# Row sums of weight tiles crossed over the partitions by a product with ones, in pairs, a pair ahead

## The chip, the cores and the metric

The kernel runs on one core of one Trainium2 chip. The metric is device time in microseconds. Before the change it took 1841.36 us (median of 3 runs, 1831.86 to 1842.78).

## The reference, cut to what matters

One layer of a streaming encoder on 1024 prompt frames and 32 running frames, 1024 channels. A normalised input is projected by a wide matrix, attention with per-head forget gates and a causal depthwise convolution of width 31 run beside each other, and both are gated, projected and added to the input.

```python
h = rmsnorm(x, norm_g)
q, k, v, f, ga, ua, ub, gb, ma, mb = split(h @ w_in)      # 1024 columns each, f: 16
u = ua * sigmoid(ub)
o = fox_attend(rmsnorm(q) / 8, rmsnorm(k), v, cumsum(log_sigmoid(f + b_f)))
conv = causal_dwconv(u, w_dw, b_dw)                        # 31 taps per channel
ya = (o * silu(ga)) @ w_pa
yb = (silu(layernorm(conv)) * silu(gb)) @ w_pb
y = x + (sigmoid(ma) * ya + sigmoid(mb) * yb) @ w_out
```

## The kernel before

Each of the groups ua, ub, ga, ma, k, q, gb, mb has eight weight tiles of 1024x128, held as 128 partitions x 1024 elements. One projection is one such tile times all 1056 frames: three chunks c of 352 frames, eight steps kt in each, and in each step three matmuls (L168), since inputs and weights are both split into a high and a low float16 part: wh·xh, wl·xh, wh·xl. One step of three matmuls is a beat; `beat()` counts ticks, runs what `later` has put off to a tick, and hands out the taps of the convolution to VectorE (L355) at a set rate per beat. A projection has 24 beats, so two have 48.

For the split to float16 each weight tile is scaled by a power of two. Four steps make it:

- `stage`: loads the tile (`raw<-wf`, L213, three buffers), and `squares` runs one pass of ScalarE over it that leaves each partition's sum of squares in `tops` (L105).
- The 128 sums lie in 128 partitions. `squares` writes them to DRAM (`s_st<-tops`, L107) and reads them back with all 128 in the row of every partition (`all<-s_st`, L110). Both DMAs are issued by SyncE (SP), whose queue issues in order.
- `sized` takes the largest on VectorE (L114); `power` makes the scale of it (L142, L143), and GpSimd its inverse (L120).
- `fetch` makes the parts: `wh` on ScalarE (L123), `wl` in three pieces on VectorE (L126).

`PREP` places `sized` and `fetch` in the first chunk (steps 3 and 5) of the projection ahead of the tile's own, and `stage` in the second chunk (step 4), for the tile after it. So a tile's sums are asked for about 15 beats after they are formed.

In order of time the program has these stages. The input is normalised and split while the first two tiles, ub and ua, are multiplied (`x_split`). Then come u1 and two quarters of v, u2 and two more quarters of v (L722, whose tiles go the same way as two raw pieces), then u3, eight pairs of k and q with u4, u5 and u6 between them, and u7. A u is the pair of projections ub and ua. Each k or q projection adds three small pairs of products with a block matrix for the norms (`pst`, L841 and L842) which wait for ScalarE (`sqh`, L831) and VectorE (`sql`, L834). Then eight projections ga. Up to there the order of TensorE, VectorE and ScalarE is that of the code; DMAs and GpSimd are placed by a scheduler. In the attention stage only TensorE has the order of the code: 16 heads of eight blocks, each with scores (L1057, L1058), maximum (L1062), exponential (L1065), scaling on GpSimd (L1068), transposes (L1082) and values (L1101), and after each block four beats of 22 filler projections (gb, ma and part of mb) whose single PSUM buffer is emptied by L897. Two more projections and the three output products follow; these don't use the scale.

Of the kernel before, what the change touches and what calls it, by code (L numbers as in the profile page):

```python
# [24 lines left out]
KT = 8  # L25
# [24 lines left out]
WSP = ((0, 3), (3, 6), (6, 8))  # L50
PREP = ((0, 3), (0, 5), (1, 4))
XCH = ((0, 256), (256, 384), (640, 416))


def build(tc, xT, xt, wv, wf, ckT, cv, clT, stT, vec, cst, yT, kT, vO, lfO, cpT, csT):
# [4 lines left out]
    def pool(name, bufs=1, stack=es, **kw):  # L60
        return stack.enter_context(tc.tile_pool(name=name, bufs=bufs, reuse_waits="tile", **kw))
# [13 lines left out]
    s_m = dram.tile([128, TT], F32, name="s_m")  # L75
    s_st = dram.tile([96, 128], F32, name="s_st")

# [13 lines left out]

    class Scaled:


        def __init__(self, raws):
            self.raws = raws
            self.sc = wx.tile([128, 4], F32, name="sc", tag="sc", bufs=8)

        def squares(self, n):
            self.n = n  # L100
            tops = wx.tile([128, 2], F32, name="tops", tag="tops", bufs=4)
            for i, raw in enumerate(self.raws):
                k = raw.shape[1] * raw.shape[2]
                junk = wx.tile([128, 4 * VC], BF16, name="junk", tag="junk", bufs=1)
                nc.scalar.activation(junk[:, :k], raw.rearrange("p a b -> p (a b)"), AF.Square,  # L105
                                     accum_out=tops[:, i:i + 1])
                nc.sync.dma_start(s_st[n + i].rearrange("(p o) -> p o", o=1), tops[:, i:i + 1])  # L107
            self.all = wx.tile([128, 256], F32, name="all", tag="all", bufs=2)
            for i in range(len(self.raws)):
                nc.sync.dma_start(self.all[:, 128 * i:128 * i + 128],  # L110
                                  s_st[n + i].rearrange("(o p) -> o p", o=1).broadcast_to([128, 128]))

        def most(self):
            nc.vector.tensor_reduce(self.sc[:, 0:1], self.all[:, :128 * len(self.raws)], axis=AX.X, op=ALU.max)  # L114
            self.power(self.sc[:, 0:1])

        def power(self, top):
            q, self.s, self.inv = [self.sc[:, i:i + 1] for i in (1, 2, 3)]
            power(q, self.s, top, 77)
            nc.gpsimd.tensor_scalar(self.inv, q, back, 1.0, op0=ALU.mult, op1=ALU.mult)  # L120

        def high(self, wh, raw, ks):
            nc.scalar.mul(wh[:, ks, :], raw[:, ks, :], self.s)  # L123

        def low(self, wl, wh, raw, ks):
            nc.vector.scalar_tensor_tensor(wl[:, ks, :], raw[:, ks, :], self.s, wh[:, ks, :],  # L126
                                           op0=ALU.mult, op1=ALU.subtract)

        def split(self):
            with tc.high_priority(offset=2000):  # L130
                raw, = self.raws
                xhome.append(xhome.pop(0))
                home = xhome[-1]
                wh, wl = [home.tile([128, KT, 128], F16, name=a, tag=a, bufs=2 if home is wp else 1) for a in ("wh", "wl")]
                self.high(wh, raw, slice(0, KT))
                for k0, k1 in WSP:
                    self.low(wl, wh, raw, slice(k0, k1))
            return wh, wl, self.inv

# [44 lines left out]
    def beat():  # L184

        pace["tick"] += 1
        while late and late[0][0] <= pace["tick"]:
            late.pop(0)[2]()
        if taps or chores:
            pace["credit"] += pace["rate"]  # L190
        while pace["credit"] >= 0 and (taps or chores):
            if chores:
                cost, fn = chores.pop(0)
                fn()
            else:
                cost = taps.pop(0)() or 1.0
            pace["credit"] -= cost

    plan = []
    staged = []  # L200
    split = {}
    serial = [0]

    def stage():

        if plan:
            key = plan.pop(0)
            with tc.high_priority(offset=2000):
                if key[0] == "v":
                    rec = Scaled(v_raws(key[1]))  # L210
                else:
                    raw = wx.tile([128, KT, 128], F32, name="raw", tag="raw", bufs=3)
                    nc.sync.dma_start(raw, wf[WIDX[key]])  # L213
                    rec = Scaled([raw])
                rec.squares(serial[0])
            serial[0] += len(rec.raws)
            staged.append((key, rec))

    def sized():

        if staged:
            with tc.high_priority(offset=2000):
                staged[0][1].most()

    def fetch():

        if staged:
            key, rec = staged.pop(0)
            split[key] = split_v(key[1], rec) if key[0] == "v" else rec.split()

    def steps(key, rh, rl, pspool, evac):

        ahead = key in split
        w = split.pop(key) if ahead else split_w(load_raw(key))
# [193 lines left out]
    with tc.high_priority(offset=9000):  # L428
# [9 lines left out]
        idle = xip.tile([128, CH], F16, name="idle")  # L438
        nc.vector.memset(idle, 0.0)
        ones_w = xip.tile([128, 128], F32, name="ones_w")  # L440
        nc.gpsimd.memset(ones_w, 1.0)
        tops = xip.tile([128, 4], F32, name="tops")
        gsq = xip.tile([128, KT], F32, name="gsq")
# [5 lines left out]
        G8 = slice(C_NG, C_NG + KT)  # L449
        recs = [Scaled([raw]) for raw in raws]  # L450
        warm = tr.tile([128, 512], F32, name="warm", tag="tr")
# [117 lines left out]
    def high(i, p):  # L569
        recs[i].high(ws0[i][0], raws[i], slice(*WSP[p]))  # L570

    def low(i, p):
        recs[i].low(ws0[i][1], ws0[i][0], raws[i], slice(*WSP[p]))

# [6 lines left out]
    def known(i):  # L581
        recs[i].power(psq[:, i + 1:i + 2])

# [29 lines left out]

    plan.extend([("ub", 1), ("ua", 1), ("v", 0), ("v", 1), ("ub", 2), ("ua", 2), ("v", 2), ("v", 3), ("ub", 3), ("ua", 3)])
    for f in range(8):
        if f in (2, 4, 6):
            plan.extend([("ub", 3 + f // 2), ("ua", 3 + f // 2)])
        plan.extend([("k", f), ("q", f)])
    plan.extend([("ub", 7), ("ua", 7)] + [("ga", f) for f in range(8)])
    fills = [("gb", f) for f in range(8)] + [(g, f) for g in ("ma", "mb") for f in range(8)]  # L620
    plan.extend(fills)
    x_split(0, ws0, u0, {
# [15 lines left out]
        6: [lambda: scale(5, 1), lambda: scale(7, 1)],  # L638
        7: [lambda: scale(8, 1), stage]})
    x_split(2, ws0, u0, {1: [stage], 3: [consts], 4: [sized], 5: [fetch], 7: [sized]})  # L640
    drain((0, 0))
# [16 lines left out]
    def v_raws(c):  # L658
        raws = [vp.tile([128, 4, VC], F32, name="vraw", tag="vraw", bufs=4) for _ in range(2)]
        for hf in range(2):  # L660
            nc.sync.dma_start(raws[hf], wv[c, :, hf * 4:hf * 4 + 4, :])
        return raws

    def split_v(c, rec):
        wh2, wl2, raws2 = [], [], rec.raws
        for raw in raws2:
            with tc.high_priority(offset=1500):
                wh, wl = [vp.tile([128, 4, VC], F16, name=a, tag=a, bufs=4) for a in ("vwh", "vwl")]
                rec.high(wh, raw, slice(0, 4))
                for k in (0, 2):  # L670
                    rec.low(wl, wh, raw, slice(k, k + 2))
            wh2.append(wh)
            wl2.append(wl)
# [25 lines left out]
    for c in range(4):  # L699
# [13 lines left out]
        pace["rate"] = R_V  # L713
        wh2, wl2, inv = split.pop(("v", c))
        for t in range(8):
            ps = pj.tile([128, 512], F32, name="pjv", tag="pj")
            n = 0
            for kt in range(KT):
# [5 lines left out]
                beat()  # L724
            for at, fn in ((1, sized), (2, fetch), (5, stage)):
                if t == at:
                    fn()
            vf = vp.tile([128, 256], F32, name="vf", tag="vf", bufs=6)
# [224 lines left out]
    psS = pool("psS", 2, stack=p2, space=PS)  # L953
    psT = pool("psT", 3, stack=p2, space=PS)
    ap = pool("ap", 2, stack=p2, side="right")

# [634 lines left out]
```

## Time and profile before

| | us |
|---|---|
| median of 3 runs | 1841.36 |
| the profiled execution | 1837.22 |
| its span | 1835.2 |
| TensorE busy | 1451.8 |
| VectorE busy | 999.2 |
| ScalarE busy | 717.7 |
| GpSimd busy | 442.2 |

The mean granted TensorE clock over the span is 0.887 of full speed. A line such as "DVE sc L114 <- DMA all<-s_st: 501.7, 64, 13.6" in the table of waits reads: VectorE's instructions of line 114 that write `sc` had their engine idle ahead of them until a DMA of `all` from `s_st` ended, 501.7 us in total in 64 cases, the longest 13.6 us. PE is TensorE, PEld its weight loads, DVE VectorE, ACT ScalarE, POOL GpSimd, SPq the queue of SyncE. A matmul's recorded duration reaches over the start of the next, so the rate of matmuls is read from their starts.

### The profile page before, as it was taken

The numbers are of one execution on the slowest core, as the hardware profiler recorded it, in microseconds if no ns is written. First come the engines' busy times: TensorE is split into PE (matmuls) and PEld (weight loads), VectorE is DVE, ScalarE is ACT, GpSimd is POOL, SyncE is SP. The second block draws the span as 40 slices with busy tenths as digits, with TensorE's granted clock in tenths as the row PEclk, the third lists the DMA queues.
The fourth block names the chain that finished last, engine by engine and source line by source line (L and its number), as shares of the span: only waits on it lengthen the run. The fifth ranks groups of instructions, "written<-read, shape, count | busy, mean of one in ns | idle before, by whom it ended". The sixth has DMA issues, their size and how long they took to land.

```text
span 1835.2 us, 25063 instructions
## 1 busy us (share of the span) xinstructions
PE 1451.8 (79%) x9344; PEld 1053.5 (57%) x9344; DVE 999.2 (54%) x1702; ACT 717.7 (39%) x1362; POOL 442.2 (24%) x505
## 2 busy tenths in 40 slices
PE   8797967767777777673676678777768699999999
PEld 5485744434444444441454455455546466999999
DVE  6575655545557676553465464544424253865575
ACT  6433335344354542212243333443424344652331
POOL 1000103122233230001222222212112122564563
PEclk8998988987799888985778888898889899999999
DMA  4442444528344336664233433534434423874453
GB/s 173 77 142 47 125 57 98 83 76 172 55 100 95 88 98 84 83 68 54 67 94 105 89 108 85 115 88 111 96 87 115 110 70 131 306 252 133 132 184 95
DMA packets 133657, 199.61 MB, mean 109 GB/s; under 512 B 45280, under 2 KB 100192, under 8 KB 133536
## 3 DMA queue, kind: packets, MB, share of 16 engines
q1 hardware_dynamic: 133392, 197.94, 44.4%
q8 instruction: 74, 1.21, 0.4%
q14 instruction: 47, 0.39, 0.1%
q10 hardware_dynamic: 144, 0.07, 0.0%
HBM read 132.27 MB, written 65.68 MB: 108 GB/s over the span
## 4 chain that ended last, share of the span: by engine, by line
DMA 47%; PE 28%; DVE 12%; ACT 7%; issue 5%; POOL 0%; SPq 0%; ACTq 0%; DVEq 0%; POOLq 0%
DMA s_st<-tops 29%; PE pj L168 16%; DMA all<-s_st 13%; PE pj L1423 4%; DMA raw<-wf 4%; DVE y L355 3%; PE pjv L722 3%; DVE wl L126 2%; ACT junk L105 2%; DVE nm L1062 2%; ACT wh L123 1%; PE ptr L1082 1%; ACT P L1065 1%; PE po L1101 1%; DVE sc L114 1%
## 5 line engine op out<-in xcount | busy, mean ns | idle before, releaser
L168 PE MATMUL pj<-xh,wh 128*128 128x352 f16 (+2 forms) x1536 | 519.9, 339 | 116.6 <-ACT t L897 54.7
L168 PE MATMUL pj<-xh,wl 128*128 128x352 f16 (+2 forms) x1536 | 518.5, 338 | 3.6 <-DVE wl L126 3.6
L168 PE MATMUL pj<-xl,wh 128*128 128x352 f16 (+2 forms) x1536 | 516.4, 336 | 2.7 <-DVE xl L557 2.4
L168 PEld LDWEIGHTS <-wh 128*128 128x128 f16 x3072 | 322.7, 105 | 259.9 <-ACT wh L123 64.3
L355 DVE SCALAR_TENSOR_TENSOR y<-u,vec_t,y 128x1086 f32<-128x1086 f32 x240 | 332.4, 1385 | 3.4 <-ACT y L352 0.4
L114 DVE TENSOR_REDUCE sc<-all 128x1 f32<-128x128 f32 (+1 forms) x67 | 19.7, 293 | 501.7 <-DMA all<-s_st 501.7
L168 PEld LDWEIGHTS <-wl 128*128 128x128 f16 x1536 | 160.9, 105 | 157.4 <-issue 63.2
L120 POOL TENSOR_SCALAR sc<-sc,back 128x1 f32<-128x1 f32 x69 | 44.7, 648 | 717.9 <-DVE sc L142 682.1
L1068 POOL TENSOR_SCALAR P<-P,nm 128x128 f32<-128x128 f32 (+7 forms) x128 | 120.5, 943 | 314.4 <-DVE nm L1067 272.2
L123 ACT ACTIVATE wh<-raw,sc 128x1024 f16<-128x1024 f32 (+1 forms) x68 | 74.4, 1095 | 306.4 <-DVE sc L143 306.4
L1065 ACT ACTIVATE P<-psS,nm 128x128 f32<-128x128 f32 (+7 forms) x128 | 94.8, 741 | 247.9 <-DVE nm L1062 190.8
L1057 PE MATMUL psS<-KB,QB 128*128 128x256 f32 (+2 forms) x192 | 89.7, 468 | 109.5 <-ACT P L1065 97.2
L126 DVE SCALAR_TENSOR_TENSOR wl<-raw,sc,wh 128x384 f16<-128x384 f32 (+1 forms) x192 | 105.5, 602 | 29.3 <-ACT wh L123 27.9
L1057 PEld LDWEIGHTS psS<-KB,QB 128*128 128x128 f32 x192 | 40.7, 212 | 129.5 <-ACT P L1065 104.9
L1082 PE MATMUL ptr<-ident,P 128*128 128x128 f32 x576 | 93.7, 294 | 9.4 <-DVE ot L1106 4.8
L1062 DVE TENSOR_REDUCE nm<-psS 128x1 f32<-128x128 f32 (+7 forms) x128 | 96.4, 754 | 7.3
L1082 PEld LDWEIGHTS ptr<-ident,P 128*128 128x128 f32 x576 | 77.2, 154 | 17.6 <-POOL P L1068 5.4
L1085 ACT COPY pt<-ptr 128x512 f32<-128x512 f32 (+3 forms) x128 | 64.2, 501 | 57.5 <-PE ptr L1082 56.5
L105 ACT ACTIVATE junk<-raw 128x1024 bf16<-128x1024 f32 x62 | 65.2, 1052 | 54.5 <-DMA raw<-wf 31.0
L859 POOL TENSOR_TENSOR ql<-qn,qh 128x352 fp32r<-128x352 f32 (+1 forms) x48 | 59.5, 1240 | 107.6 <-ACT qh L858 74.5
L722 PE MATMUL pjv<-vwh,xh 128*128 128x260 f16 x256 | 72.2, 282 | 14.3 <-ACT vwh L123 12.5
L160 POOL TENSOR_TENSOR wl<-raw,wh 128x384 fp32r<-128x384 f32 (+1 forms) x51 | 63.1, 1265 | 74.6 <-ACT wh L157 58.8
(266 smaller groups left out, 2628.8 us busy)
## 6 DMA issues: line engine op xcount, KB each, us to landing
raw<-wf SPq DMA_DIRECT2D x92, 512.0 KB
QB<-s_q SPq DMA_DIRECT2D x32, 256.0 KB
KB<-s_k SPq DMA_DIRECT2D x32, 256.0 KB
all<-s_st SPq DMA_DIRECT2D x70, 64.0 KB
kT<-qn SPq DMA_DIRECT2D x8, 528.0 KB
s_ga<-t SPq DMA_DIRECT2D x24, 176.0 KB
s_gb<-t SPq DMA_DIRECT2D x24, 176.0 KB
s_ma<-t SPq DMA_DIRECT2D x24, 176.0 KB
```

What stands on the lines that cost most here:

```text
L105: nc.scalar.activation(junk[:, :k], raw.rearrange("p a b -> p (a b)"), AF.Square, accum_out=tops[:, i:i + 1])
L123: nc.scalar.mul(wh[:, ks, :], raw[:, ks, :], self.s)
L126: nc.vector.scalar_tensor_tensor(wl[:, ks, :], raw[:, ks, :], self.s, wh[:, ks, :], op0=ALU.mult, op1=ALU.subtract)
L168: nc.tensor.matmul(ps, a[:, kt, :], b(kt, sl), start=(first and n == 0), stop=(last and n == N - 1))
L355: t = nc.vector.scalar_tensor_tensor(y, u[:, i:i + CW], w, y, op0=ALU.mult, op1=ALU.add)
L722: nc.tensor.matmul(ps[:, :VC], a, b, start=(n == 0), stop=(n == 23))
L1057: nc.tensor.matmul(ps[:, b, :wm], QB[:, qsl], KB[:, ksl], start=True, stop=False)
L1062: nc.vector.tensor_reduce(nm[:, 0:1], ps[:, :nb, :w], axis=AX.XY, op=ALU.max, negate=True)
L1065: nc.scalar.activation(P[:, :nk].rearrange("p (b w) -> p b w", b=nb), ps[:, :nb, :w], AF.Exp, bias=nm[:, 0:1], accum_out=nm[:, 1:2])
L1068: nc.gpsimd.tensor_scalar(P[:, :nk], P[:, :nk], nm[:, 2:3], 1.0, op0=ALU.mult, op1=ALU.mult)
L1082: nc.tensor.transpose(pt[:, 128 * j:128 * j + 128], P[:, 128 * (4 * u + j):128 * (4 * u + j) + 128], ident)
L1423: nc.tensor.matmul(pss[c][:, :HC], a[:, k, :], x, start=(not more and kt == 0 and n == 0), stop=(kt == 3 and n == 2), skip_group_check=more)
```

## The change

The class `Scaled` becomes `Batch`, which stands for two tiles (a quarter of v: one batch of two raw pieces with one common scale). The sums of squares go to `topb` in bfloat16 on GpSimd, and `total` multiplies a matrix of ones with them on TensorE, which leaves in each partition the sum over all 128 partitions. `power` reads that from PSUM for both tiles at once. The scale thus follows from the total and not from the largest partition. `s_st`, `all` and the maximum go. Where the old kernel had three marks in each projection, `begin` at the start of a pair lists the jobs for the next pair with their ticks, and `beat` runs them. There are four raw buffers.

```diff
-            for i, raw in enumerate(self.raws):
...
-                nc.sync.dma_start(s_st[n + i].rearrange("(p o) -> p o", o=1), tops[:, i:i + 1])
-            self.all = wx.tile([128, 256], F32, name="all", tag="all", bufs=2)
-            for i in range(len(self.raws)):
-                nc.sync.dma_start(self.all[:, 128 * i:128 * i + 128],
-                                  s_st[n + i].rearrange("(o p) -> o p", o=1).broadcast_to([128, 128]))
-
-        def most(self):
-            nc.vector.tensor_reduce(self.sc[:, 0:1], self.all[:, :128 * len(self.raws)], axis=AX.X, op=ALU.max)
-            self.power(self.sc[:, 0:1])
+            raw = wx.tile([128, KT, 128], F32, name="raw", tag="raw", bufs=4)
+            nc.sync.dma_start(raw, wf[WIDX[key]])
...
+                    nc.scalar.activation(junk[:, :raw.shape[1] * raw.shape[2]], raw.rearrange("p a b -> p (a b)"),
+                                         AF.Square, accum_out=self.tops[:, i:i + 1])
+                if len(self.raws) == 2:
+                    nc.gpsimd.tensor_copy(self.topb, self.tops)
+
+        def total(self):
+            pool, tag = totals[-1]
+            self.ps = pool.tile([128, 512], F32, name="tot", tag=tag)
+            if self.n == 2:
+                nc.tensor.matmul(self.ps[:, :2], ones_b, self.topb, start=True, stop=True)
+            else:
+                for i in range(2):
+                    nc.tensor.matmul(self.ps[:, 0:1], ones_b, self.topb[:, i:i + 1], start=(i == 0), stop=(i == 1))
+
+        def power(self, ps=None, n=0):
+            ps, n = (self.ps, self.n) if ps is None else (ps, n)
+            with tc.high_priority(offset=2000):
+                q, self.s, self.inv = [self.sc[:, 2 * i:2 * i + n] for i in range(3)]
+                power(q, self.s, ps[:, :n], 77)
+                nc.gpsimd.tensor_scalar(self.inv, q, back, 1.0, op0=ALU.mult, op1=ALU.mult)
...
     def beat():
 
         pace["tick"] += 1
+        while prep and prep[0][0] <= pace["tick"]:
+            prep.pop(0)[1]()
...
+    def begin():
+
+        if not plan:
+            return
+        b = plan.pop(0)()
+        t = pace["tick"]
+        if b.n == 2:
+            jobs = ((3, b.stage), (13, b.stage), (25, b.total), (27, b.power), (29, lambda: b.split(0)),
+                    (40, lambda: b.split(1)))
+        else:
+            jobs = ((3, b.stage), (25, b.total), (27, b.power),
+                    (29, lambda: split.__setitem__(b.keys[0], split_v(b.keys[0][1], b))))
+        prep.extend((t + n, fn) for n, fn in jobs)
...
-                if ahead and (c, kt) in PREP:
-                    (sized, fetch, stage)[PREP.index((c, kt))]()
```

In `x_split` the first pair is loaded and squared at the end of the second chunk and the start of the third, its total follows at step 3 and its splits at steps 5 and 7 of the third chunk. In the attention stage `tot` takes one of the three PSUM buffers of the transposes (`psT`), before that the single buffer `tr`.

VectorE, in the pairs of k and q; before, the maximum of the sums, the scale and three pieces of `wl` of one tile:

```order
L355 SCALAR_TENSOR_TENSOR y<-u,vec_t,y 128x1086
L114 TENSOR_REDUCE sc<-all 128x1
L142 TENSOR_SCALAR sc<-sc 128x1
L143 TENSOR_SCALAR sc<-sc 128x1
L126 SCALAR_TENSOR_TENSOR wl<-raw,sc,wh 128x384 x2
L126 SCALAR_TENSOR_TENSOR wl<-raw,sc,wh 128x256
L848 SCALAR_TENSOR_TENSOR qn<-pj,gi,ri 128x352
```

The same engine after the change, in a later pair of k and q (the lines on `ls`, `csm`, `ch` and `cl` are the small work on the forget gates that falls there):

```order
L158 TENSOR_SCALAR sc<-tot 128x2
L159 TENSOR_SCALAR sc<-sc 128x2
L813 COPY ls<-lfT 16x32
L142 SCALAR_TENSOR_TENSOR wl<-raw,sc,wh 128x384 x2
L142 SCALAR_TENSOR_TENSOR wl<-raw,sc,wh 128x256
L814 SCALAR_TENSOR_TENSOR csm<-on_3443,ls 16x544
L864 SCALAR_TENSOR_TENSOR qn<-pj,gi,ri 128x352
L850 TENSOR_TENSOR sql<-sqf,sqh 128x352
L816 CAST ch<-cc 16x1024
L864 SCALAR_TENSOR_TENSOR qn<-pj,gi,ri 128x352
L817 TENSOR_TENSOR cl<-cc,ch 16x1024
L142 SCALAR_TENSOR_TENSOR wl<-raw,sc,wh 128x384 x2
```

The reduction is gone, the scale comes once for two tiles from `tot` in PSUM, and the two tiles' `wl` stand apart.

SyncE's queue in a pair of k and q, before:

```order
L861 DMA s_k<-ql 128x352
L213 DMA raw<-wf 128x1024
L860 DMA s_k<-qh 128x352
L107 DMA s_st<-tops 128x1
L861 DMA s_k<-ql 128x352
L864 DMA kT<-qn 128x1056
L110 DMA all<-s_st 128x128
L860 DMA s_k<-qh 128x320
L861 DMA s_k<-ql 128x320
```

And after:

```order
L877 DMA s_k<-ql 128x352
L107 DMA raw<-wf 128x1024
L876 DMA s_k<-qh 128x352
L877 DMA s_k<-ql 128x352
L880 DMA kT<-qn 128x1056
L876 DMA s_k<-qh 128x320
L107 DMA raw<-wf 128x1024
L877 DMA s_k<-ql 128x320
```

The write of the sums and their reading back have left the queue, and a second tile is loaded within the same stretch.

TensorE after the change, at the 25th beat of a pair (before, only the rows of L184, then L168, stood there):

```order
L184 MATMUL pj<-xl,wh 128x352
L126 LDWEIGHTS ones_b
L126 MATMUL tot<-topb,ones_b 128x2
L184 LDWEIGHTS wh
L184 MATMUL pj<-xh,wh 128x352
```

One product with its weight load has come into TensorE's own stream; there are 31 such for pairs and two for each of the four quarters of v.

More of the change, by code (lines that the diff above doesn't have):

```diff
@@ L75, in build @@
     s_m = dram.tile([128, TT], F32, name="s_m")
-    s_st = dram.tile([96, 128], F32, name="s_st")
     cp = pool("cp")
@@ L136, in split @@
                 for k0, k1 in WSP:
-                    self.low(wl, wh, raw, slice(k0, k1))
-            return wh, wl, self.inv
+                    self.low(i, wl, wh, raw, slice(k0, k1))
+            split[self.keys[i]] = wh, wl, self.inv[:, i:i + 1]
     def power(q, s, top, e):
@@ L199, in build @@
     plan = []
-    staged = []
     split = {}
[L202 to L229, printed above, removed]
+    prep = []
+    totals = []
+    def begin():
[10 more added lines that the diff above has]
+        prep.extend((t + n, fn) for n, fn in jobs)
     def steps(key, rh, rl, pspool, evac):
-        ahead = key in split
-        w = split.pop(key) if ahead else split_w(load_raw(key))
+        if key in firsts:
+            begin()
+        w = split.pop(key) if key in split else split_w(load_raw(key))
         for c in range(3):
@@ L439, in build @@
         nc.vector.memset(idle, 0.0)
+        ones_b = cp.tile([128, 128], BF16, name="ones_b")
+        nc.vector.memset(ones_b, 1.0)
         ones_w = xip.tile([128, 128], F32, name="ones_w")
         nc.gpsimd.memset(ones_w, 1.0)
-        tops = xip.tile([128, 4], F32, name="tops")
+        tops = xip.tile([128, 4], F32, name="tops0")
         gsq = xip.tile([128, KT], F32, name="gsq")
@@ L449, in build @@
         G8 = slice(C_NG, C_NG + KT)
-        recs = [Scaled([raw]) for raw in raws]
+        recs = [Batch((i,)) for i in range(2)]
         warm = tr.tile([128, 512], F32, name="warm", tag="tr")
@@ L638, in build @@
         6: [lambda: scale(5, 1), lambda: scale(7, 1)],
-        7: [lambda: scale(8, 1), stage]})
-    x_split(2, ws0, u0, {1: [stage], 3: [consts], 4: [sized], 5: [fetch], 7: [sized]})
+        7: [lambda: scale(8, 1), b1.stage]})
+    x_split(2, ws0, u0, {0: [b1.stage], 2: [consts], 3: [b1.total, b1.power], 5: [lambda: b1.split(0)],
+                         7: [lambda: b1.split(1)]})
     drain((0, 0))
@@ L668, in split_v @@
                 wh, wl = [vp.tile([128, 4, VC], F16, name=a, tag=a, bufs=4) for a in ("vwh", "vwl")]
-                rec.high(wh, raw, slice(0, 4))
+                rec.high(0, wh, raw, slice(0, 4))
                 for k in (0, 2):
-                    rec.low(wl, wh, raw, slice(k, k + 2))
+                    rec.low(0, wl, wh, raw, slice(k, k + 2))
             wh2.append(wh)
@@ L714, in build @@
         wh2, wl2, inv = split.pop(("v", c))
+        begin()
         for t in range(8):
@@ L954, in build @@
     psT = pool("psT", 3, stack=p2, space=PS)
+    totals.append((psT, "T"))
     ap = pool("ap", 2, stack=p2, side="right")
```

84 lines of the change are left out of this document (48 added, 36 removed).

## The prediction

> **What bounds the kernel now.** I read the page's chain first, then the table of waits, one round of the timeline, and last the busy times by stage. The page:
>
> ```profile
> span 1835.2 us, 25063 instructions
> DMA 47%; PE 28%; DVE 12%; ACT 7%; issue 5%; POOL 0%; SPq 0%; ACTq 0%; DVEq 0%; POOLq 0%
> DMA s_st<-tops 29%; PE pj L168 16%; DMA all<-s_st 13%; PE pj L1423 4%; DMA raw<-wf 4%; DVE y L355 3%; PE pjv L722 3%; DVE wl L126 2%; ACT junk L105 2%; DVE nm L1062 2%; ACT wh L123 1%; PE ptr L1082 1%; ACT P L1065 1%; PE po L1101 1%; DVE sc L114 1%
> L114 DVE TENSOR_REDUCE sc<-all 128x1 f32<-128x128 f32 (+1 forms) x67 | 19.7, 293 | 501.7 <-DMA all<-s_st 501.7
> L120 POOL TENSOR_SCALAR sc<-sc,back 128x1 f32<-128x1 f32 x69 | 44.7, 648 | 717.9 <-DVE sc L142 682.1
> ```
>
> 42% of the chain that ends last is two tiny DMAs, the write of the row sums and their reading back, and VectorE stands 501.7 us ahead of the 67 maxima. Those waits block a queue in order: every tap, eviction and maximum behind L114 waits too. The table of waits shows who pays, and that SyncE is blocked by the same write:
>
> ```profile
> ACT wh L123 <- DVE sc L143: 306.4, 41, 13.9
> PE psS L1057 <- ACT P L1065: 97.2, 18, 10.2
> PE pst L841 <- ACT sqh L831: 44.7, 14, 7.0
> PE pst L842 <- DVE sql L834: 39.7, 17, 5.7
> SPq L110 <- DMA s_st<-tops: 499.3, 69, 9.6
> ```
>
> One round in order of time (start, duration, engine; in brackets the idle time before):
>
> ```profile
> 461.71 0.32 SPq L107 DMA_DIRECT2D s_st<-tops  x1
> 471.38 0.32 SPq L110 DMA_DIRECT2D all<-s_st  x1
> 471.75 0.31 PE L168 MATMUL pj<-xl,wh 128*128 128x352 f16 x1
> 474.71 0.29 DVE L114 TENSOR_REDUCE sc<-all 128x1 f32<-128x128 f32 x1 [8.20 <-DMA all<-s_st]
> 475.40 1.15 ACT L123 ACTIVATE wh<-raw,sc 128x1024 f16<-128x1024 f32 x1 [5.93 <-DVE sc L143]
> 476.61 0.47 PE L168 MATMUL pj<-xh,wh 128*128 128x352 f16 x1 [4.54 <-ACT wh L123]
> 477.82 0.50 PE L168 MATMUL pj<-xh,wh 128*128 128x352 f16 x1
> 478.11 0.50 PE L168 MATMUL pj<-xh,wl 128*128 128x352 f16 x1
> ```
>
> The write takes 471.38 - 461.71 = 9.67 us, the reading back 474.71 - 471.38 = 3.33, together 13.0. TensorE has used up its tile, waits 4.54 us for the next, and then runs at a start distance of 0.29 us. Busy times by stage (length, then PE, PEld, DVE, ACT, POOL, granted clock, DMA share, GB/s):
>
> ```profile
> 0.00:55.20 55.20, 46.14 (x256) 29.39 (x257) 31.44 (x85) 31.26 (x65) 8.26 (x21) 0.91 0.40 145
> 55.20:133.90 78.70, 69.62 (x562) 53.12 (x560) 49.73 (x66) 30.63 (x66) 6.04 (x7) 0.96 0.46 114
> 133.90:217.30 83.40, 71.57 (x565) 53.92 (x563) 53.37 (x66) 32.04 (x71) 6.35 (x7) 0.94 0.33 95
> 217.30:691.40 474.10, 353.27 (x1979) 213.60 (x1977) 281.10 (x414) 204.16 (x366) 120.15 (x122) 0.86 0.44 93
> 691.40:828.00 136.60, 101.39 (x578) 60.39 (x578) 77.04 (x100) 32.53 (x51) 9.21 (x10) 0.87 0.64 73
> 828.00:1544.00 716.00, 522.62 (x3445) 363.76 (x3445) 329.98 (x747) 275.89 (x597) 144.10 (x218) 0.85 0.38 92
> 1500.00:1544.00 44.00, 43.71 (x360) 30.62 (x360) 20.02 (x46) 20.27 (x44) 7.95 (x13) 1.00 0.15 49
> 1544.00:1565.00 21.00, 21.00 (x143) 13.78 (x142) 9.35 (x16) 11.29 (x14) 5.43 (x6) 1.00 0.87 307
> 1565.00:1835.00 270.00, 266.23 (x1829) 265.48 (x1826) 167.17 (x211) 99.90 (x136) 142.67 (x114) 1.00 0.55 180
> ```
>
> They are x_split; u1 with half of v; u2 with the rest; u3 to u7 with k and q; ga; attention; its last 44 us, where no tile is prepared any more; the last two gates; the output products. Where no sums are fetched TensorE is busy 99 to 100% at clock 1.00. Where they are, it is busy 73 to 75% at 0.85 to 0.87, and no engine is full. So the round trip bounds everything from 55 to some 1465 us.
>
> **The floor.** What would TensorE alone need? 143 matmuls in 21.00 us are 0.147 us each, so a projection of 72 takes 10.6 us. The products of float32 operands at the end run at 270 / 1829 = 0.148; six of them for the norms make a k or q 11.5. For v and the attention:
>
> ```profile
> 107.30 24.95 PE pjv L722 x224
> 1473.75 0.64 PE L1057 MATMUL psS<-KB,QB 128*128 128x256 f32 x1
> 1500.04 0.31 PE L168 MATMUL pj<-xh,wh 128*128 128x352 f16 x1 [0.25 <-ACT t L897]
> 1501.92 1.08 PE L990 MATMUL psS<-kc,qs_t 64*32 64x512 f32 x8
> 1502.80 0.26 PE L991 MATMUL psS<-ks_t,qs_t 64*32 64x32 f32 x8
> 1505.48 0.41 PE L1057 MATMUL psS<-KB,QB 128*128 128x256 f32 x1
> ```
>
> A quarter of v is 192 matmuls at 24.95 / 224 = 0.111, 21.4 us. From the second block of one head to that of the next, after the last wait for sums, go 1505.48 - 1473.75 = 31.7 us, with one of the four groups of running frames in them. So 16 heads take at most 508. Such a group's scores take about 1.1 us (L990 and L991), its transposes and 20 small products some 2 more, an estimate; 12 heads have none, which gives 508 - 36 = 472, and I use 470. Floors by stage: u1 and half of v 21.2 + 42.8 = 64, the same again 64, u3 to u7 with k and q 5 x 21.2 + 16 x 11.5 = 290, ga 85, attention 470.
>
> **The change part by part.**
>
> *The round trip goes.* All 501.7 us of waits on VectorE and 499.3 on SyncE lose their cause, and 67 maxima of 0.293 us go. The Trainium skill's DMA: Bandwidth & Descriptors ("Anatomy of one DMA") gives about 2.0 us of fixed cost to a DMA. Two would be 4.0 us, less than the some 15 beats (15 x 3 x 0.147 = 6.6 us) that the old order leaves them, and the change would gain nothing: 1835. The trace, with 9.67 and 3.33, disagrees, and it decides.
>
> What is late next? In u3 to q7 VectorE: from its 281.10 I take 24 times a maximum and about half the scale work, some 0.4 each, and 270 us are left beside TensorE's 290. An engine in order that is 93% loaded delivers late at times. Of the 84.4 us that L841 and L842 wait now I let half stay, and add 8 for the tiles: 340. ScalarE's 204.16 leave it room. In ga VectorE keeps about 74 of 85: 97.
>
> *Total on TensorE.* 35 batches (31 pairs and four quarters), one or two products each, in TensorE's own queue: behind a waiting total every projection stands. The nearest rows, a product with ones of the first stage, and one load of a tile in the attention with the ScalarE pass that waited for it:
>
> ```profile
> L458 PE MATMUL pj<-tops,ones_w x6: 167/260/353, 5.2 to 12.1; 128*128 128x1 f32 x6
> 865.31 0.33 SPq L213 DMA_DIRECT2D raw<-wf  x1
> 869.91 1.06 ACT L105 ACTIVATE junk<-raw 128x1024 bf16<-128x1024 f32 x1 [0.86 <-DMA raw<-wf]
> ```
>
> Below, 0.26 us a batch, 9 in all; nothing speaks for a gain of its own. Above, the total waits for a load only now issued: 4.60 + 1.06 + 0.65 for the copy on GpSimd (by L120, mean 0.648) + 0.26 = 6.6 us, 230 in all. Between second stage and total lie twelve beats, 5.3 us, and with four buffers the load can start before its stage; SyncE's new order has it there. So I take it nearer to the lower end, some 1.5 us a batch, 35 of them 52 us, which lie within the additions of this sum.
>
> *Pairs.* Both splits stand 19 and 8 beats, 8.4 and 3.5 us, ahead of the pair's end, the second not needed for 24 beats more. In the attention ScalarE makes both `wh` in a row and VectorE six pieces of `wl`, ahead of a block's maximum. For this and the totals I add 45 us there, 3.75 for each of the 12 batches: 515. The first totals add 7 and 5 in the stages of v, where a quarter's load stands behind the stores of u0 in SyncE's queue: 71 and 69. If the cover of twelve beats fails, it is the 230 above. The copy of two numbers on GpSimd and the third and fourth buffer cost nothing that is waited for: GpSimd is busy 120.15 of 474.10 us.
>
> *x_split* has one wait for sums in it and one at its end, which go:
>
> ```profile
> 49.39 0.29 DVE L114 TENSOR_REDUCE sc<-all 128x1 f32<-128x128 f32 x1 [4.11 <-DMA all<-s_st]
> 60.12 0.28 DVE L114 TENSOR_REDUCE sc<-all 128x1 f32<-128x128 f32 x1 [6.19 <-DMA all<-s_st]
> ```
>
> Of their 10.3 us I take 7 off this stage: 48.
>
> Sum: 48 + 71 + 69 + 340 + 97 + 515 + 21 + 270 = 1431 us, against floors of 48 + 64 + 64 + 290 + 85 + 470 + 21 + 270 = 1312. With the 2 us by which the execution (1837.22) exceeds its span: 1433. The median of the runs stands 0.2% above the profiled execution, so 1436; I say 1435.
>
> **The rivals.**
>
> 1. *Nearly the floor.* The pairs hide all; 1312 + 35 = about 1350. For it: 99% busy in 1500 to 1544. Against: no tile is prepared there, and VectorE has 20.02 of 44 to do, not 93%.
>
> 2. *Small waits keep the clock down.* With VectorE and ScalarE closely behind TensorE, a product for the norms, an eviction or a total waits 1 to 2 us a few times in each pair, and the granted clock stays at 0.86 as now. Then 290, 85 and 470 become 845 / 0.86 = 983, 138 more, and with 60 of waits 1312 + 198 = 1510. Against: at 1500.04 a wait of 0.25 left the clock at 1.00. The Trainium skill's TensorE: Matmul & The Clock Gate ("A second HAM failure mode: psum-queue depth-cycling") says that short idle spells between groups of matmuls, as buffers are cycled, let the clock swing. By it the sum would be this rival's 1510; the row of 1500.04 does not bear it out, for waits that short.
>
> 3. *The total is a new wait in full.* 230 us on TensorE, 1312 + 230 + 60 = 1600.
>
> 4. *Slower.* SyncE issues in order. If in the attention a tile's load stands behind a load of V that waits for TensorE's values, while TensorE stands at that tile's total, each batch costs a round of three engines. Slower than now begins where a batch costs (1835 - 1312) / 35 = 15 us, 1850 at 15.4. That is longer than the longest wait of `wh` for its scale, 13.9 us, at every one of 35 batches, and the DMA engines are rid of two transfers a tile.
>
> 5. *The round trip was hidden anyway*, no change: the 4.54 us of TensorE at 476.61, and 306.4 us of `wh`, speak against it.
>
> **How the numbers follow.** Forecast (1375 to 1490) 0.56; near the floor 0.13; small waits 0.17; totals in full 0.08; slower 0.04; no change 0.02. 1345 to 1560 holds the forecast, the second rival, and most of the first: a little over 0.8. Within 1% is about what a measurement here can't tell from no change. Faster by over 1%: 0.56 + 0.13 + 0.17 + 0.08 = 0.94; within 0.02; slower 0.04.
>
> **What would show it.** In the profile of the changed kernel: no `s_st` or `all`; VectorE's idle time ahead of L158 below 60 us in all; TensorE's idle time ahead of the totals (L126, L129) below 60, against some 230 in the third rival; a granted clock of 0.95 or more over the whole span, against 0.86 to 0.90 in the second; u3 to q7 in 310 to 370 us with `pst` as its first waiter; a head of attention in 29 to 34 us. I am wrong if a new wait of TensorE over 100 us appears on one line, or if the stages from 55 us on shrink by less than 300 us together.

## The result and the profile after

The changed kernel took 1402.55 us (median of 4 runs, 1402.31 to 1402.74), beside 1842.07 for the kernel before. The ratio is 0.762 with an interval of 0.760 to 0.765: 24% faster. Of two kernels further down, the unused round trip and the late pairs, only the profiled run is used, since the other run of each was disturbed.

The page of the changed kernel's profiled run (1402.74 us; mean granted clock 0.983):

```profile
span 1401.0 us, 24783 instructions
PE 1331.1 (95%) x9383; PEld 1008.6 (72%) x9383; DVE 983.2 (70%) x1572; ACT 723.8 (52%) x1362; POOL 428.6 (31%) x508
PE 75%; DVE 10%; DMA 6%; ACT 5%; issue 3%; POOL 0%; SPq 0%; ACTq 0%; DVEq 0%; POOLq 0%
```

The chain that ended last was 47% DMA and 28% TensorE; it is now 6% DMA and 75% TensorE. VectorE and ScalarE have nearly the same busy time as before (983.2 and 723.8 us, against 999.2 and 717.7): their work has not become cheaper, they only no longer stand still. The table of waits of the same run, TensorE's, VectorE's on the totals, and those of SyncE's queue:

```profile
PE pst L858 <- DVE sql L850: 24.1, 7, 8.1
PE pj L184 <- ACT t L913: 15.6, 17, 4.7
PE psS L1074 <- ACT P L1082: 10.5, 5, 6.3
DVE sc L158 <- PE tot L126: 18.6, 9, 4.6
DVE sc L158 <- PE tot L129: 2.0, 2, 1.1
SPq L914 <- ACT t L913: 149.2, 40, 9.3
SPq L107 <- DVE wl L142: 138.1, 42, 30.2
```

Where VectorE waited 501.7 us for the sums read back, it waits about 21 for totals. SyncE's longest wait is now for data to be stored (L914, an evicted gate) or for a raw buffer to come free (L107, by the last `wl` that reads it) (the longest of 30.2 us); TensorE's own waits for what lies behind them are the small ones above. Busy times by stage, same columns and stages as in the prediction, without its row for the attention's last 44 us:

```profile
0.00:52.10 52.10, 43.43 (x257) 28.12 (x258) 32.86 (x88) 32.57 (x66) 8.51 (x22) 0.97 0.47 172
52.10:119.30 67.20, 66.56 (x567) 52.15 (x565) 54.13 (x63) 31.63 (x66) 2.05 (x8) 1.00 0.47 150
119.30:186.20 66.90, 66.90 (x570) 52.52 (x569) 48.99 (x57) 33.21 (x71) 4.01 (x9) 1.00 0.30 99
186.20:519.50 333.30, 308.57 (x1993) 200.42 (x1992) 278.28 (x367) 205.77 (x369) 114.56 (x117) 0.96 0.40 124
519.50:606.70 87.20, 86.51 (x583) 56.67 (x581) 75.67 (x83) 37.56 (x57) 6.99 (x16) 1.00 0.36 121
606.70:1109.50 502.80, 471.71 (x3455) 339.26 (x3455) 316.26 (x691) 271.83 (x586) 142.75 (x216) 0.98 0.45 124
1109.50:1130.50 21.00, 21.00 (x143) 13.81 (x142) 9.46 (x16) 11.29 (x14) 5.44 (x6) 1.00 0.86 300
1130.50:1401.00 270.50, 266.44 (x1829) 265.66 (x1826) 167.51 (x211) 99.96 (x136) 144.27 (x114) 1.00 0.56 180
```

| stage | before | predicted | after |
|---|---|---|---|
| x_split | 55.2 | 48 | 52.1 |
| u1, u2 and v | 162.1 | 140 | 134.1 |
| u3 to u7 with k, q | 474.1 | 340 | 333.3 |
| ga | 136.6 | 97 | 87.2 |
| attention | 716.0 | 515 | 502.8 |
| last gates, output products | 291.0 | 291 | 291.5 |
| sum | 1835.0 | 1431 | 1401.0 |

The two stages in which nothing was changed stand still; the gain lies in the others. The clock goes with it: in the stages of v and ga TensorE is now busy 99 to 100% and the granted clock is 1.00, where it was 0.87 to 0.96.

The preparation of one pair of k and q in order of time, picked from the timeline (start, duration, engine):

```profile
377.99 0.33 SPq L107 DMA_DIRECT2D raw<-wf  x1
384.16 0.33 SPq L107 DMA_DIRECT2D raw<-wf  x1
384.65 1.05 ACT L117 ACTIVATE junk<-raw 128x1024 bf16<-128x1024 f32 x1
390.24 1.04 ACT L117 ACTIVATE junk<-raw 128x1024 bf16<-128x1024 f32 x1
393.32 1.28 POOL L120 CAST topb<-tops 128x2 bf16<-128x2 f32 x1
395.52 0.31 PE L184 MATMUL pj<-xl,wh 128*128 128x352 f16 x1
395.67 0.17 PE L126 MATMUL tot<-topb,ones_b 128*128 128x2 bf16 x1
395.70 0.31 PE L184 MATMUL pj<-xh,wh 128*128 128x352 f16 x1
396.97 0.15 DVE L158 TENSOR_SCALAR sc<-tot 128x2 int32<-128x2 int32 x1
397.16 0.17 DVE L159 TENSOR_SCALAR sc<-sc 128x2 int32<-128x2 int32 x1
398.11 1.13 ACT L139 ACTIVATE wh<-raw,sc 128x1024 f16<-128x1024 f32 x1
```

Each load is issued 6 to 7 us ahead of the pass that reads it, and neither pass has to wait. The second row sum was ready at 391.38, when ScalarE's accumulator had been read behind the pass shown, the copy of both at 394.60, and the total goes through TensorE at 395.67 between two matmuls that start 0.18 us apart, against 0.15 elsewhere. From the sums to VectorE's first use of the total the crossing takes 396.97 - 391.38 = 5.6 us, where it took 13.0; some 3 of them are slack ahead of the copy and of the product, TensorE spends 0.17, and in this pair neither TensorE nor VectorE waits for any of it.

### The profile page after: what moved, and what is told of

The parts are those of the page before. It is cut to its first block, busy times and chain, and to the rows that moved or that the text cites. A ratio compares the mean times of both kernels' runs of the same rounds, so it can differ in the third digit from the quotient of the medians.

```text
span 1401.0 us, 24783 instructions
## 1 busy us (share of the span) xinstructions
PE 1331.1 (95%) x9383; PEld 1008.6 (72%) x9383; DVE 983.2 (70%) x1572; ACT 723.8 (52%) x1362; POOL 428.6 (31%) x508
## 4 chain that ended last, share of the span: by engine, by line
PE 75%; DVE 10%; DMA 6%; ACT 5%; issue 3%; POOL 0%; SPq 0%; ACTq 0%; DVEq 0%; POOLq 0%
PE pj L184 50%; PE pjv L741 6%; PE pj L1440 5%; PE po L1118 4%; DMA raw<-wf 4%; DVE y L359 4%; PE ptr L1099 3%; PE psS L1074 2%; DVE nm L1079 2%; PE psS L1075 2%; DVE wl L142 2%; ACT P L1082 1%; ACT wh L139 1%; ACT t L913 1%; PE pst L858 1%
## 5 line engine op out<-in xcount | busy, mean ns | idle before, releaser
L184 PE MATMUL pj<-xh,wh 128*128 128x352 f16 (+2 forms) x1536 | 487.0, 317 | 17.7 <-ACT t L913 15.6
L184 PE MATMUL pj<-xl,wh 128*128 128x352 f16 (+2 forms) x1536 | 485.6, 316 | 1.4 <-DVE xl L563 1.1
L184 PE MATMUL pj<-xh,wl 128*128 128x352 f16 (+2 forms) x1536 | 486.1, 316 | 0.3 <-DVE wl L142 0.3
L184 PEld LDWEIGHTS <-wh 128*128 128x128 f16 x3072 | 304.1, 99 | 164.8 <-issue 4.3
L184 PEld LDWEIGHTS <-wl 128*128 128x128 f16 x1536 | 152.0, 99 | 93.4 <-issue 21.9
L1082 ACT ACTIVATE P<-psS,nm 128x128 f32<-128x128 f32 (+7 forms) x128 | 94.8, 741 | 71.9 <-DVE nm L1079 59.0
L1074 PE MATMUL psS<-KB,QB 128*128 128x256 f32 (+2 forms) x192 | 81.5, 426 | 13.9 <-ACT P L1082 10.5
L120 POOL CAST topb<-tops 128x2 bf16<-128x2 f32 x35 | 15.1, 432 | 233.6 <-ACT junk L117 180.1
L117 ACT ACTIVATE junk<-raw 128x1024 bf16<-128x1024 f32 x62 | 65.2, 1051 | 31.9 <-DMA raw<-wf 31.5
L1084 DVE RECIPROCAL nm<-nm 128x1 f32<-128x1 f32 x128 | 20.5, 160 | 77.8 <-ACT P L1082 76.8
L1118 PE MATMUL po<-pt,V 128*64 128x256 f32 x640 | 72.8, 382 | 0.0
L1077 DVE TENSOR_TENSOR psS<-psS,cmask 128x128 f32<-128x128 f32 x128 | 37.5, 294 | 47.4 <-PE psS L1075 47.0
```

The source lines that it names most:

```text
L184: nc.tensor.matmul(ps, a[:, kt, :], b(kt, sl), start=(first and n == 0), stop=(last and n == N - 1))
L1074: nc.tensor.matmul(ps[:, b, :wm], QB[:, qsl], KB[:, ksl], start=True, stop=False)
L1082: nc.scalar.activation(P[:, :nk].rearrange("p (b w) -> p b w", b=nb), ps[:, :nb, :w], AF.Exp, bias=nm[:, 0:1], accum_out=nm[:, 1:2])
L1118: nc.tensor.matmul(po[rows], V[:, j, :], parts[c][:, j, :], start=(c % 2 == 0 and j < 2), stop=(c % 2 == 1 and j >= 2 * c))
```

## The experiments

Theory A was that the exchange of the crossing carries the whole gain, and that pairs, the pair ahead and the buffers are worth next to nothing by themselves. Against it stood that the larger lead of the pairs hides the round trip, so that it matters little how the sums cross. Within A a second question was open: is it VectorE's waiting for the sums that cost the time, or SyncE's queue, which stands at each store until it has landed (A2)? All kernels compute the whole reference.

### The crossing alone, and the pairs alone

The kernel before, with only the crossing exchanged; single tiles, three buffers and the old marks stay:

```diff
-                nc.sync.dma_start(s_st[n + i].rearrange("(p o) -> p o", o=1), tops[:, i:i + 1])
...
+            nc.gpsimd.tensor_copy(self.topb[:, :m], tops[:, :m])
+
+        def total(self):
...
+            for i in range(m):
+                nc.tensor.matmul(self.ps[:, 0:1], ones_b, self.topb[:, i:i + 1], start=(i == 0), stop=(i == m - 1))
...
-            nc.vector.tensor_reduce(self.sc[:, 0:1], self.all[:, :128 * len(self.raws)], axis=AX.X, op=ALU.max)
-            self.power(self.sc[:, 0:1])
+            self.power(self.ps[:, 0:1])
```

> The kernel before with only the crossing exchanged: product with ones in place of the two DMAs and the maximum; single tiles, three raw buffers and the old marks stay (sums asked for 15 beats after they are formed). Theory A, the round trip itself is what cost: Square 1.05, copy 0.2 to 1.3 and product 0.2 us fit into 15 beats (6.6 us), so nearly the whole gain is here: 1400 to 1440 us. Theory B, the pairs and their place a pair ahead are what hides it: a good part of the gain is missing, 1500 us or more.

It took 1399.26 us (1398.39 to 1402.06), ratio 0.767 (0.765 to 0.769). The changed kernel, run again on another chip beside the kernel before, took 1402.68, ratio 0.769 (0.766 to 0.772).

> The changed kernel unaltered, for comparison on this chip: 1395 to 1410 us.

The crossing alone gives the whole gain, just below the range that theory A gave. The view of its line of totals:

```profile
L116 PE MATMUL tot<-topb,ones_b x71: 163/167/178, 43.5 to 1106.8; 128*128 128x1 bf16 x71
  DVE xl L565: 1.2, 2
  POOL topb L109: 0.5, 1
```

71 totals instead of 39, and TensorE stood ahead of them 1.7 us in all. Its old marks leave some 15 beats between sums and total, and that suffices too. By stage the two kernels are not alike: u3 to u7 take 325.1 us with single tiles and 333.3 with pairs, the attention 507.7 and 502.8, so the pairs lose 8 us in the one stage and gain 5 in the other.

The other half: the changed kernel with the two DMAs and the maximum put back, in pairs, a pair ahead, four buffers:

```diff
+                    nc.sync.dma_start(s_st[serial[0]].rearrange("(p o) -> p o", o=1), self.tops[:, i:i + 1])
+                    nc.sync.dma_start(self.all[:, i, :],
+                                      s_st[serial[0]].rearrange("(o p) -> o p", o=1).broadcast_to([128, 128]))
...
-                nc.tensor.matmul(self.ps[:, :2], ones_b, self.topb, start=True, stop=True)
...
+                        nc.vector.tensor_reduce(ps, self.all, axis=AX.X, op=ALU.max)
```

> The changed kernel with the two DMAs and the maximum put back in place of the product; pairs, their ticks and four raw buffers stay. Theory A: the second tile's sums are asked for 14 beats (6.2 us) after they are formed and need some 13 us, so VectorE waits 5 to 8 us for each of 35 batches and the clock falls behind each: 1600 to 1720 us. Theory B: being a pair ahead hides most of it: 1420 to 1480 us.

1779.86 us, ratio 0.975 (0.972 to 0.979), and so above the 1600 to 1720 that theory A had left to it; beside the kernel before it is 2 to 3% less. From its table of waits:

```profile
DVE mx L135 <- DMA all<-s_st: 288.3, 28, 18.0
ACT wh L143 <- DVE sc L163: 208.9, 20, 18.5
SPq L122 <- DMA s_st<-tops: 492.3, 67, 10.0
```

The maxima now come once for two tiles and VectorE waits 28 times for pairs, and four times for quarters of v (35.8 us, L137), instead of 64 times for both, yet 324 of 501.7 us are left, and SyncE's wait is as long as it was (499.3). The pair is a pair ahead only at its end: from the second stage at tick 13 to the maximum at tick 27 there are 14 beats, no more than the 15 before. So I asked whether a longer lead would hide it:

```diff
-            jobs = ((3, b.stage), (13, b.stage), (25, b.total), (27, b.power), (29, lambda: b.split(0)),
-                    (40, lambda: b.split(1)))
+            jobs = ((1, b.stage), (5, b.stage), (25, b.total), (38, b.power), (40, lambda: b.split(0)),
+                    (44, lambda: b.split(1)))
```

> As pairs_alone, but stages at ticks 1 and 5 and the maximum at tick 38: 33 beats (14.5 us at full rate) between the second sums and their use, more than the 13 us of the round trip. If VectorE's wait and SyncE's are two costs that add, VectorE's falls away and SyncE's 190 us stay: 1580 to 1640 us. If the second write queues behind the first read back, so that a pair needs two round trips in a row (some 22 us): VectorE still waits 5 us or more for each pair, 1680 us or more.

1657.63 us in one run, beside 1822.97 for the kernel before on that chip. Its waits:

```profile
DVE mx L135 <- DMA all<-s_st: 158.6, 17, 17.8
SPq L122 <- DMA s_st<-tops: 396.6, 57, 10.4
```

33 beats of lead instead of 14, and VectorE's wait for the pairs is nearly halved, not gone: neither expectation held. SyncE's row says why, I think, though no run shows it alone: the reading back stands in its queue behind the store, and everything else, other sums too, stands behind the reading.

### Which of the waits cost the time

The changed kernel, whose scale comes from the total, with the round trip made for nobody: both DMAs as above, `all` unread. VectorE doesn't wait for it; SyncE does.

> The changed kernel that also writes the sums to DRAM and reads them back, for nobody: the scale still comes from the product. It keeps SyncE's wait of some 9 us for each of 70 tiles and the DMA engines' load, and takes VectorE's wait away. Theory A1, VectorE's wait was the cost: 1405 to 1450 us. Theory A2, SyncE's blocked queue was a cost of its own (loads, stores and buffers behind it come late): 1500 to 1700 us.

1591.38 us in one run, beside 1826.42: two DMAs whose result no engine uses put it some 189 us above the changed kernel. From its page (the chain by line) and its table of waits:

```profile
PE pj L191 27%; DMA s_st<-tops 6%; PE pjv L748 5%; PE pj L1447 5%; DMA s_y<-y 4%; DVE y L366 4%; DMA raw<-wf 4%; DMA s_ga<-t 4%; PE po L1125 3%; DVE wl L149 2%; PE ptr L1106 2%; DVE nm L1086 2%; PE psS L1081 1%; DMA s_q<-qh 1%; ACT P L1089 1%
```

```profile
SPq L123 <- DMA s_st<-tops: 502.6, 66, 10.0
DVE y L336 <- DMA s_y<-y: 74.9, 7, 23.2
PE pst L865 <- DVE sql L857: 44.7, 10, 17.8
PE pst L864 <- ACT sqh L854: 26.9, 10, 9.5
PE psS L1081 <- ACT t L918: 24.0, 1, 24.0
```

SyncE stands at the reading back until the store has landed, 502.6 us as in the kernel before. What is queued behind it, the stores of the convolution (`s_y`) and of the gates (`s_ga`) and the loads of tiles, comes late, and through their buffers VectorE, ScalarE and at last TensorE. The same kernel without the reading back shows what the stores alone cost, with nobody waiting for them:

```diff
+                    nc.sync.dma_start(s_st[serial[0]].rearrange("(p o) -> p o", o=1), self.tops[:, i:i + 1])
```

> As unused_trip, but without the reading back: the 4-byte writes of the sums stay (load of the DMA engines), SyncE no longer waits for them. If the queue's wait was what cost some 190 us in unused_trip: 1402 to 1420 us. If the writes hold up the DMA engines for everything else: 1500 us or more.

1466.09 us (1460.28 to 1471.90), ratio 0.804 (0.798 to 0.810): 63 us more than the changed kernel on the same chip (1402.68), which neither expectation had. From its page, and then from that of the changed kernel, the DMA packets and the queue that carries them (with the chain by engine in the first):

```profile
DMA packets 123575, 195.00 MB, mean 134 GB/s; under 512 B 44160, under 2 KB 90112, under 8 KB 123456
q1 hardware_dynamic: 123312, 193.35, 50.5%
PE 65%; DMA 13%; DVE 11%; ACT 6%; issue 3%; POOL 1%; SPq 0%; ACTq 0%; DVEq 0%; POOLq 0%
```

```profile
DMA packets 113495, 194.96 MB, mean 139 GB/s; under 512 B 34080, under 2 KB 80032, under 8 KB 113376
q1 hardware_dynamic: 113232, 193.31, 44.9%
```

70 stores of 128 x 4 bytes, 36 KB in all, add 144 packets each, and raise the time that the packets take from 0.449 x 1401.0 = 629 us on each of the 16 engines to 0.505 x 1458.5 = 737, some 108 more. The records of q1's single packets in the two traces show whose time that is. All packets of 4 bytes together take 7.8 us on each engine in the changed kernel and 16.0 here, a single one 9 ns (median) in both. The rest of the rise lies in other packets: 132 of them took over 1 us in the changed kernel, 10.5 us on each engine, and 806 here, 110.3 us, the longest 8.1; all others together take 610 us in both. So the stores cost the DMA engines little by themselves; other transfers were held up. That goes with the stores in every profile here: the five kernels that have them show 313 to 933 such packets, the nine without 123 to 155. And SyncE is not free of them either. In the table of its queue's waits it now stands at the stores until ScalarE has formed the sums:

```profile
SPq L121 <- ACT junk L119: 102.0, 49, 17.3
```

Whether the 63 us come from the transfers held up or from this wait in the queue, no run separates. Its windows for u3 to u7 and for the attention show where the 58 us of span went:

```profile
185.87:551.29 365.42, 316.02 (x1992) 202.40 (x1990) 273.61 (x365) 204.84 (x369) 107.68 (x117) 0.94 0.51 113
639.00:1166.80 527.80, 483.97 (x3454) 346.05 (x3453) 315.60 (x691) 271.55 (x586) 141.08 (x216) 0.95 0.48 119
```

32 in the first and 25 in the second, with the clock at 0.94 and 0.95. DMA has 13% of the chain, against 6% in the changed kernel.

So the steps add up: 1403 with the total on TensorE; + 63 for the stores alone; + 125 where SyncE also reads back and must wait for them (1591); + 189 where VectorE waits for the result too (1780); + 46 with single tiles in the old order (1826). They come from two chips, on which the kernel before took 1823 and 1826 us, and two of the steps rest on the one run of 1591, while the two runs of the stores alone lie 12 us apart; I take each step as good to some 15 us, an estimate. The step of 125 has the packets of the reading back in it. The packets' time on each engine is no larger there (0.451 x 1589.6 = 717 us, against 737), which speaks for the wait, but no run has the reading back without it. Both readings of A had a part: with the causes taken away in this order, VectorE's wait was about half of the 377 us from 1403 to 1780, SyncE's wait to read back a third, the stores a sixth.

### Buffers and cover

Two raw buffers instead of four (`bufs=4` becomes `bufs=2` for `raw`):

> The changed kernel with two raw buffers in place of four, so a tile's load starts only once the tile of the pair before is split. If twelve beats between second stage and total and some 19 between split and next stage (8 us, against 4.6 us for a load) are cover enough: 1400 to 1412 us, no wait of TensorE for a total. If the four buffers carry the change: ScalarE stands at the load, the totals wait, 1440 us or more.

1405.37 us (1403.11 to 1407.68), ratio 0.770 (0.768 to 0.772), which can't be told from the changed kernel. The waits show the small price:

```profile
ACT junk L117 <- DMA raw<-wf: 57.6, 26, 6.1
PE tot L126 <- POOL topb L120: 4.1, 1, 4.1
```

ScalarE waits 57.6 us for tiles instead of 31.5, and one total had TensorE waiting. The prediction's cover of twelve beats, cut to six (`(25, b.total)` becomes `(19, b.total)`):

> The changed kernel with the total six beats (2.6 us) behind the second stage, not twelve. By the prediction's upper bound (the total waits for a load only now issued, 6.6 us): 4 us of wait for most of 31 pairs, 1490 us or more. If the load has long landed, only Square 1.05 and copy 0.2 to 1.3 us are ahead of it: 1400 to 1425 us, TensorE's idle time ahead of L126 below 25 us.

1403.93 us (1401.05 to 1406.81), ratio 0.763 (0.760 to 0.765). TensorE's wait for the totals:

```profile
PE tot L126 <- POOL topb L120: 6.8, 4, 2.0
```

Six beats are enough, within 7 us, as the second expectation had it. Where a total would begin to hurt wasn't tried.

### What is late next

TensorE's first wait is that of the norms' products for VectorE's `sql` (24.1 us). They are put off by 11 ticks after the projection's chunk; here by 14, and by 17:

```diff
-            later(11, lambda: root(c, sl, ps, sqh, sql))
+            later(14, lambda: root(c, sl, ps, sqh, sql))
```

> The changed kernel with the products for the norms put off to 14 beats behind their eviction (11 before). They are now the first wait of TensorE from u3 to q7 (24.1 us at the second product of the pair). If that wait is only lateness of VectorE: 10 to 25 us less than the changed kernel on the same chip. If VectorE's load is what binds there: within 5 us of it.

> The changed kernel with the products for the norms at 17 beats. If lateness of VectorE is all that is left there, 0 to 8 us less than root_later (1389 to 1397); if PSUM buffers held longer become a wait, more than 1397.

By 14: 1396.71 us (1392.62 to 1400.06), ratio 0.765 (0.761 to 0.769). That is 6 us less than the changed kernel on that chip, between the two expectations. By 17: 1392.57 (1392.51 to 1392.63), ratio 0.757 (0.755 to 0.759). In the second u3 to u7 take 321 us instead of 333, and the waits have gone down with them:

```profile
PE pst L858 <- DVE sql L850: 10.1, 3, 5.3
```

At 14 the interval still overlaps that of the changed kernel; at 17 it doesn't. This is the fastest version measured, 0.7% below the changed kernel. Two more runs ask whether it is VectorE's load that binds there, and whether the old single tiles go as well with the later products. The first hands out fewer taps of the convolution in k and q and more in v and ga:

```diff
-R_U, R_V, R_QK, R_G, R_A = 0.21, 0.145, 0.16, 0.23, 0.2
+R_U, R_V, R_QK, R_G, R_A = 0.21, 0.16, 0.14, 0.25, 0.2
```

> root_later with the rate of convolution taps moved from the pairs of k and q (0.16 to 0.14 a beat) to v (0.145 to 0.16) and ga (0.23 to 0.25), where VectorE has more room. If VectorE's load of 83% in u3 to q7 is what TensorE waits for there: 5 to 15 us less than root_later, 1382 to 1392; if not, the same as root_later.

1396.24 us (1394.83 to 1397.93), ratio 0.759 (0.757 to 0.760): the time that 14 ticks had without it, on another chip, and u3 to u7 take 327 us in both. But the traces show that the edit moved little: three of 105 taps, and VectorE's busy time in that stage went from 272.94 to 270.87 us, while ga grew from 86.3 to 91.1. So this run doesn't settle whether VectorE's load matters there. The second is the crossing alone with 14 ticks:

> crossing_alone with the products for the norms at 14 beats. If pairs and four buffers carry nothing, it is like root_later: 1388 to 1402 us.

1398.49 us (1396.59 to 1401.27), ratio 0.760 (0.758 to 0.762): no more and no less than the pairs with 14, as expected if pairs and buffers carry nothing.

## Why the prediction was right, and where its sizes were off

- **What bounds.** "The round trip bounds everything from 55 to some 1465 us" held: the crossing alone is the whole gain. That the same waits block a queue in order held for VectorE and for SyncE. The prediction priced no share for the two; the runs give about half to VectorE, a third to SyncE's wait to read back and a sixth to the stores. The 2.0 us that it sets against the trace stand in the Trainium skill's DMA: Bandwidth & Descriptors ("Anatomy of one DMA") under DMAs issued by GpSimd; these two were SyncE's, and the sum went by the trace's 9.67 and 3.33.
- **The floor.** Last gates and output products came at 21.0 and 270.5, as taken over. The floors of the v stages and of ga, 64, 64 and 85, were missed by some 3 us each or less; TensorE stands idle 0.7 us or less in each of them.
- **VectorE late in u3 to q7.** Right in mechanism and nearly in size: 333.3 us for 340. The norms' wait was put at half of 84.4 and came out as 24.1, the first of TensorE's waits as foretold. VectorE's load is 278.28 us for the 270 taken. That the moment at which the product asks for `sql` costs is what the run with 17 ticks speaks for: with nearly the same load (272.77 us) the stage is 12 us shorter. That VectorE's load has no part in it isn't shown.
- **Total on TensorE.** The mechanism was right, the size was not: 1.5 us for each of 35 batches, 52 in all, measured 1.4 (both parts ahead of the totals of v, L129; none ahead of those of pairs, L126). The 1.5 was a choice between 0.26 and 6.6 us, whose upper bound came from a load that is only now issued. With the sums ready 4 us ahead the value was at the lower end, 0.17 us a product: 39 x 0.167 = 6.5 us. It is a term that was mis-sized, and it is part of the additions to the stages: in the attention 45 became 502.8 - 470 = 32.8, in ga 12 became 2.2, in the v stages 12 became 6.1. What is left in the attention is not totals: TensorE is idle 502.8 - 471.7 = 31.1 us there, most of it ahead of filler projections for an eviction (L913, 15.6) and of scores for an exponential (L1082, 10.5).
  The view of line L129 in the changed kernel, with the products (ns: shortest, median, longest) and the idle time ahead of them (us, times); the same view of L126 has 31 products of 167 ns and no such row:

```profile
L129 PE MATMUL tot<-topb,ones_b x8: 163/164/167, 64.1 to 150.8; 128*128 128x1 bf16 x8
...
  issue: 0.8, 1
  POOL topb L120: 0.6, 1
```

- **x_split** was missed the other way: 7 of 10.3 us were taken off, and 3.1 came off. Of the two waits counted there only the first, 4.11 us ahead of 49.39, lies in the stage; of the second, 6.19 us ahead of 60.12, all but 1.3 us stand behind its end at 55.20, in the next stage.
- **Sum.** 1431 forecast, 1401.0 measured: -4.1 + 5.9 + 6.7 + 9.8 + 12.2 - 0.5 = 30 us by stage, 2%.
- **Rival 1** (the floor, 1350), **rival 3** (230 us of totals) and **rival 5** (no change) are refuted. **Rival 2** is too: waits of several us are left (up to 8.1 at L858 and 6.3 at L1074), and yet the clock is 0.96 and 0.98 in their stages, not 0.86; it is 1.00 in the v stages and ga, where TensorE stands idle 0.7 us or less in each. By the Trainium skill's TensorE: Matmul & The Clock Gate ("A second HAM failure mode: psum-queue depth-cycling") frequent short idle spells would let it swing; the trace agrees only by the 2 to 4% that the clock lost in those two stages. **Rival 4**, a total that holds up the round of three engines, had no place: the longest wait for a total's operand that any run here shows is 4.1 us, in two_raws.
- **The pairs** were treated as cover that the total needs. crossing_alone shows that it needs no pairs: the old 15 beats of lead suffice, and six did in total_19.

## What to carry to other kernels

Where a few numbers must cross the partitions, price the route by what it does to the queues it passes, not by its own length: a store and a reading back through DRAM cost here 377 us, and about half of it was the engine that wanted the numbers. A product with ones on an engine that is busy anyway cost 0.17 us and needed neither pairs nor a fourth buffer, and no more lead than the six beats that were tried. Where a rework brings several edits together, run the smallest of them alone: here it gave all the gain.

## What was not expected of the hardware

- Seventy stores of 128 times 4 bytes cost 63 us though no engine used what they wrote: 10,080 packets, 36 KB. The Trainium skill's DMA: Bandwidth & Descriptors ("Why small descriptors are slow (HBM only)") gives an overhead of some 3 cycles to a packet; with one for the data, an estimate by it, 10,080 packets on 16 engines are 2,520 cycles on each. The trace has 8.2 us on each for them (16.0 - 7.8). So the packets' own overhead is not what was dear: the other 99 of the 108 us fell on other packets, some 670 of which were held up for over 1 us. Why they were held up no run here shows.
- More than twice the lead did not hide a round trip of 13 us: from 14 to 33 beats (33 x 3 x 0.147 = 14.6 us) VectorE's wait for the pairs fell only from 288.3 to 158.6 us.
